# Prompt attention: value products of two steps taken in one visit of TensorE's 64-column arrangement

## The chip, the cores and the metric

The kernel runs on one core of a Trainium2 chip. A core has TensorE (PE in the profile; its weight loads are PEld), VectorE (DVE), ScalarE (ACT), GpSimd (POOL) and SyncE (SP), which issues most transfers. Each runs its own list of instructions in order and waits for the others through semaphores. The metric is the device time of one execution in microseconds; shorter is better.

## The reference

One inference step of a decoder layer for 1024 prompt tokens and 32 sample tokens. The part that matters here is the causal attention of the prompt: 8 heads, keys and queries of 96 numbers, values of 64, queries in blocks of 128.

```python
def masked_attend(q, k, v, q_pos, k_pos):
    s = jnp.einsum('...qhd,...khd->...hqk', q, k).astype(jnp.float32) * (QK_HEAD ** -0.5)
    s = jnp.where(k_pos[None, :] <= q_pos[:, None], s, NEG_INF)
    p = jax.nn.softmax(s, axis=-1).astype(v.dtype)
    return jnp.einsum('...hqk,...khd->...qhd', p, v)
```

Around it stand the projections, a gated mixer, attention of the sample tokens over a paged cache, cross-attention into 256 memory tokens, and a gated feed-forward part. All is float32; most matmuls are made of three products of a high and a low part.

## The kernel before

`phase2a` (L673) holds the prompt's attention. It is cut into 16 units (L721 and L722), numbered 0 to 15 here, each one head `h` and one half `G` of the tokens: four query blocks `e` of 128 tokens. With G = 0 a unit is short: its keys reach over 1 to 4 blocks, and it has three steps. With G = 1 it is long: 5 to 8 blocks, four steps (L997). In their order the units are (0,0), (1,0), (0,1), (1,1), (2,0), (2,1), (3,0), (3,1), (4,0), (4,1), (5,0), (6,0), (5,1), (7,0), (6,1), (7,1) as (h, G). So units 0, 1, 4, 6, 8, 10, 11 and 13 are short.

Of a unit, `scores` (L999) makes the scores of one query block on TensorE and VectorE takes them from PSUM with the mask and the maximum (L1015, L1019, L1021). `expo` (L1023) is ScalarE's exponential. `trans` (L1028) transposes the probabilities of one bank, four blocks of 128x128, on TensorE (L1032), and ScalarE copies them into a `pth` tile (L1034), of which there are six. `value` (L1036) multiplies a bank with the values (L1047): the stationary operand has 64 columns, the even query blocks' result goes to the first 64 partitions of the PSUM tile `o`, that of the odd ones to the other 64. A short unit has three banks, one in each step; a long one has seven, two in each of the first three steps and one in the last. `copy` (L1052) takes `o` to SBUF on VectorE, `out` (L1057) transposes it back, and VectorE scales it (L1064).

The order of TensorE, ScalarE, VectorE and GpSimd is written out by hand (L782 to L844). One step runs, in this order:

- in a unit's last step the exponentials that are pending
- `T`: the transposes of the step's banks (L811)
- the `out` that is due, then the other pending exponentials
- `jobs`: scores of the next unit's query blocks, or of the one after it (L818)
- `V`: the value products of the step before (L823 and L824), so a step's banks are transposed in one step and multiplied in the next
- `extra`: projections and head preparations (`proj_group`, `head_prep`, L985), weight sums on GpSimd, and steps that prepare the sample tokens

A *visit* here is a run of value products between other matmuls. The scores of a unit's last query block come one or two steps before the unit's own first step, since its first transposes need all four exponentials. Each bank's products accumulate into the unit's `o`, from its first bank to its last.

Of the kernel before, what the change touches and what calls it, by code (L numbers as in the profile page):

```python
# [154 lines left out]
class Net:  # L155
# [517 lines left out]
    def phase2a(self):  # L673
# [77 lines left out]
        for h in range(2, 8):  # L751
            b = 7 * (h - 1)
# [12 lines left out]
        def sample():  # L765
            self.close("lat")
            yield from self.sample_prep(pp)
            yield from self.pages_ahead()

        def mix():  # L770
            n = [self.t(p, [P, 4, 4, 96], F32, r, 2).rearrange("p m h d -> p (m h d)") for r in "kq"]
            hl = [x[:, 512:].rearrange("p (k n) -> p k n", k=4) for x in n]
            for k, _ in enumerate(self.mix_steps(
                pm, pp, 1, 0, 4, lambda i: b_all[:, i], lambda j: hl[j], lambda j: n[j // 2][:, :512], ("tp", 4)
            )):
                if k not in (1, 2, 8):
                    yield
                if k == 4:
                    yield

        E = mybir.EngineType
        with tc.manual_schedule(engines={E.PE, E.Activation, E.DVE, E.Pool}):  # L782
            for f in preps[0][0], preps[0][1], v1[0], norm[0], norm[1]:
                f()
            self.lows = []
            preps[1][0]()
            for e in range(4):
                units[0]["a"](e)
                if e == 1:
                    preps[1][1]()  # L790
                if e:
                    units[0]["e"](e - 1)
                    if e % 2:
                        v1[e // 2 + 1]()
            units[0]["e"](3)
            for f in norm[2:4]:
                f()
            self.flush()
            extra[0][:0] = norm[4:]
            extra[1][:0] = v1[3:]  # L800
            steps, outs, pend, V = [], {}, [], []
            self.sums = []
            t = 0
            for n, u in enumerate(units):
                for k, banks in enumerate(u["steps"]):
                    self.flush()
                    if k == len(u["steps"]) - 1:
                        for f in pend:
                            f()
                        pend = []  # L810
                    for b in banks:  # L811
                        u["T"](b)
                    for f in outs.pop(t, []):
                        f()
                    for f in pend:
                        f()
                    pend = []
                    for w, e in jobs[t]:  # L818
                        w["a"](e)
                        pend.append(lambda w=w, e=e: w["e"](e))  # L820
                    self.flush()
                    self.flush_sums()
                    for f in V:  # L823
                        f()  # L824
                    V = [lambda u=u, b=b: u["V"](b) for b in banks]
                    if k == len(u["steps"]) - 1:
                        outs.setdefault(t + 2, []).append(u["copy"])
                        outs.setdefault(t + 3, []).append(u["out"])
                        if order[n] == (7, 0):
                            outs[t + 3].append(lambda: steps.append(mix()))  # L830
                    for f in extra[t]:
                        f()
                    t += 1
                    if t == 32:
                        steps.append(sample())
                    steps = [x for x in steps if next(x, 0) is None]
            self.flush()
            self.flush_sums()
            self.lows = self.sums = None
            for fs in [V] + [outs[t] for t in sorted(outs)] + [[]] * 4:  # L840
                for f in fs:
                    f()
                steps = [x for x in steps if next(x, 0) is None]
            assert not steps  # L844
# [146 lines left out]
    def head_unit(self, p, pp, h, G, s, c):  # L991
# [75 lines left out]

        u.update({"a": scores, "e": expo, "T": trans, "V": value, "copy": copy, "out": out})
        return u
# [1443 lines left out]
```

## Time and profile before

| what | value |
|---|---|
| runs, median of 3 | 1827.49 us (1826.86 to 1828.1) |
| span of the profiled execution, first to last instruction | 1823.1 us |
| median of the runs less that span | 4.4 us |
| granted TensorE clock, mean | 0.998 |
| VectorE, ScalarE, GpSimd busy | 74%, 51%, 39% |
| value products L1047: records, first and last start | 352, 208.0 to 397.9 us |
| transposes L1032 and copies L1034 of them | 288 and 80 |

The profile gives the span of its execution; the times of the runs also hold what lies before the first instruction and after the last. Each value product shows as two records of TensorE. Rows of the timeline are: start in us from the span's start, length in us, engine, line, operation, out<-in, shapes, how many in a row, and in brackets the idle time before it and what ended it. Matmuls overlap and their lengths are modelled, so work on TensorE is best read from one start to the next. The table by stretches gives the stretch, its length, busy time and instructions of PE, PEld, DVE, ACT and POOL, then the granted TensorE clock, the DMA share and GB/s.

### The profile page before, as it was taken

To read this page: it belongs to the slowest core of one execution; us is meant where nothing else is said; L and a number is where in the kernel's file an instruction comes from. 1 tells how busy PE (TensorE), PEld (TensorE's weight loads), DVE (VectorE), ACT (ScalarE), POOL (GpSimd) and SP (SyncE) were. 2 spreads that over 40 slices of the span, in tenths; PEclk is the share of its full clock that TensorE was granted. 3 is DMA by queue.
4 is the path that set the end of the run, shared out by engine and by line. 5 is a ranking of instruction groups with operands and counts; after the bars stand their busy time and mean duration, and the time that the engine had idled before them with its cause. 6 is when DMAs were issued, how large, how long until landed. Compare 5 with 4: busy or idle time off the path is not lost.

```text
span 1823.1 us, 39307 instructions
## 1 busy us (share of the span) xinstructions
PE 1800.6 (99%) x14226; PEld 1700.3 (93%) x14226; DVE 1349.6 (74%) x2796; ACT 921.5 (51%) x1910; POOL 703.0 (39%) x861
## 2 busy tenths in 40 slices
PE   9999999999999999999999999999999999999999
PEld 8999777779999999998899979999999999999999
DVE  7864767657778776777645767998888888888664
ACT  7435676766655555556433556533333333344442
POOL 1021655534545444544023010377667776400000
PEclk9999999999999999999999999999999999999999
DMA  8102354558866766664645156222222222595242
GB/s 323 47 18 70 117 176 127 165 181 227 220 201 189 202 189 181 178 180 127 194 152 188 36 197 196 71 71 94 83 71 71 83 71 85 152 325 162 85 149 78
DMA packets 153187, 261.18 MB, mean 143 GB/s; under 512 B 20897, under 2 KB 97538, under 8 KB 152994
## 3 DMA queue, kind: packets, MB, share of 16 engines
q1 hardware_dynamic: 152130, 257.63, 45.4%
q8 instruction: 112, 1.84, 0.4%
q10 hardware_dynamic: 864, 1.05, 0.2%
q14 instruction: 81, 0.66, 0.1%
HBM read 212.79 MB, written 45.82 MB: 142 GB/s over the span
## 4 chain that ended last, share of the span: by engine, by line
PE 81%; DVE 3%; ACT 1%; issue 1%; SPq 1%; POOL 1%; DMA 0%; DVEq 0%; ACTq 0%; POOLq 0%
PE s L186 22%; PE d L186 12%; PE b L186 8%; PE F L186 7%; PE X L186 7%; PE E L186 7%; PE A L186 3%; PE y L186 3%; PE o L1047 2%; PE o L1537 2%; PE tp L1032 1%; PE tp L186 1%; PE s L1422 1%; PE tp L985 1%; PE t L186 1%
## 5 line engine op out<-in xcount | busy, mean ns | idle before, releaser
L186 PE MATMUL s<-w2h,ch 128*128 128x256 f32 x1018 | 301.9, 297 | 0.5 <-ACT S L1425 0.5
L186 PE MATMUL s<-w2h,cl 128*128 128x256 f32 x1018 | 293.2, 288 | 0.0
L186 PE MATMUL s<-w2l,ch 128*128 128x256 f32 x1018 | 292.9, 288 | 0.0
L186 PEld LDWEIGHTS s<-w2h,ch 128*128 128x128 f32 x1018 | 191.5, 188 | 8.9 <-issue 3.7
L186 PEld LDWEIGHTS s<-w2l,ch 128*128 128x128 f32 x1018 | 191.7, 188 | 0.0
L186 PEld LDWEIGHTS s<-w2h,cl 128*128 128x128 f32 x1018 | 191.3, 188 | 0.0
L1458 DVE TENSOR_REDUCE ss<-sq 128x16 f32<-128x1024 f32 x128 | 155.3, 1213 | 29.8 <-ACT sq L1455 29.4
L1407 POOL TENSOR_TENSOR cl<-cT,ch 128x512 fp32r<-128x512 f32 x64 | 83.5, 1304 | 185.6 <-ACT ch L1403 185.4
L1455 ACT ACTIVATE sq<-s 128x512 f32<-128x512 f32 x128 | 76.6, 598 | 82.7 <-PE s L186 82.7
L1452 ACT ACTIVATE sq<-s 128x512 f32<-128x512 f32 x128 | 76.9, 601 | 75.9 <-PE s L186 70.9
L201 ACT CAST a<-brb 128x528 fp32r<-128x528 f32 x77 | 48.8, 634 | 110.5 <-PE d L186 104.6
L186 PE MATMUL d<-a,w 128*128 128x264 f32 x768 | 95.2, 284 | 0.0
L202 DVE TENSOR_TENSOR a<-brb,a 128x528 fp32r<-128x528 f32 x77 | 54.1, 704 | 55.2 <-ACT a L201 55.1
L186 PEld LDWEIGHTS d<-a,w 128*128 128x128 f32 x768 | 94.3, 188 | 0.0
L2149 POOL TENSOR_TENSOR lo<-s,hi 128x1024 fp32r<-128x1024 f32 x20 | 64.0, 3200 | 45.7 <-ACT hi L2148 45.7
L186 PE MATMUL mm<-whi,xh 128*128 128x256 f32 (+3 forms) x272 | 77.1, 285 | 0.0
L2204 ACT COPY a<-A 128x264 f32<-128x264 f32 x43 | 16.1, 375 | 120.6 <-PE A L186 114.2
L186 PE MATMUL mm<-wlo,xh 128*128 128x256 f32 (+3 forms) x272 | 76.8, 285 | 0.1
L186 PE MATMUL mm<-whi,xl 128*128 128x256 f32 (+3 forms) x272 | 76.8, 286 | 0.0
L1403 ACT CAST ch<-cT 128x512 fp32r<-128x512 f32 x128 | 73.5, 629 | 0.0
L2270 POOL TENSOR_TENSOR cv<-cv,row 128x1056 f32<-128x1056 f32 x22 | 65.1, 2960 | 21.0 <-ACT cv L2269 21.0
L186 PE MATMUL d<-a,hi 128*128 128x264 f32 x552 | 72.0, 284 | 0.0
(755 smaller groups left out, 6348.1 us busy)
## 6 DMA issues: line engine op xcount, KB each, us to landing
cT<-cT SPq DMA_DIRECT2D x256, 160.0 KB, 2.8
ck<-ck SPq DMA_DIRECT2D x256, 144.0 KB, 3.4
raw<-w_up SPq DMA_DIRECT2D x44, 512.0 KB, 3.5
wsumd<-wsum SPq DMA_DIRECT2D x26, 512.0 KB, 3.9
actd<-cv SPq DMA_DIRECT2D x44, 264.0 KB, 2.4
brb<-actd SPq DMA_DIRECT2D x44, 264.0 KB, 5.7
wsum<-w_down SPq DMA_DIRECT2D x22, 512.0 KB, 3.8
raw<-wsumd SPq DMA_DIRECT2D x20, 512.0 KB, 3.7
```

The source lines that it names most:

```text
L186: x = self.nc.tensor.matmul(out, l, r, start=first and i == 0, stop=last and i == len(seq) - 1)
L201: first = {"act": nc.scalar.copy, "pool": nc.gpsimd.tensor_copy, "dve": nc.vector.tensor_copy}[eng](hi, src)
L202: low = lambda: nc.vector.tensor_tensor(lo, src, hi, ALU.subtract)
L1047: nc.tensor.matmul(u["o"][g : g + 64, o : o + m * P], s["v"][:, j, h % 4], th[:, z * P : (z + m) * P], start=j == 0, stop=b == len(banks) - 1,
L1403: nc.scalar.copy(d["h"][:, k], src[k])
L1407: (nc.vector if k else nc.gpsimd).tensor_tensor(d["l"][:, k], src[k], d["h"][:, k], ALU.subtract)
L1452: nc.scalar.activation(sq[:, 0], ps[:, :, n0 : n0 + 256], AF.Square)
L1455: nc.scalar.activation(sq[:, 1], pt.rearrange("p (e d) -> p e d", e=2), AF.Square)
L1458: yield lambda: nc.vector.tensor_reduce(s["ss"][:, g0 : g0 + 2].rearrange("p e (z h) -> p z e h", z=2), sq.rearrange("p z e (h d) -> p z e ...
L1537: nc.tensor.matmul(s["o"][j * 32 : j * 32 + 32], S[:, q * 4 + j], d["ck"][:, j, :257], start=q == 0 and j > 0, stop=q == 7)
L2149: eng.tensor_tensor(lo, src, hi, ALU.subtract)
L2270: nc.gpsimd.tensor_tensor(cv, cv, row, ALU.mult)
```

## The change

The list `V` of value products is no longer run in every step. It is run in the first step of a unit (k = 0), and in a long unit also in its third (k = 2); between those, the products of further steps are appended to it. A long unit's banks 0 to 3 are multiplied in its third step and its banks 4 to 6 in the first step of the next unit; a short unit's three banks all in the first step of the next unit, after that step's transposes and scores. What is left after the last unit is run at the end as before.

```diff
@@ -820,9 +820,11 @@
                         pend.append(lambda w=w, e=e: w["e"](e))
                     self.flush()
                     self.flush_sums()
-                    for f in V:
-                        f()
-                    V = [lambda u=u, b=b: u["V"](b) for b in banks]
+                    if k == 0 or k == 2 and len(u["steps"]) == 4:
+                        for f in V:
+                            f()
+                        V = []
+                    V += [lambda u=u, b=b: u["V"](b) for b in banks]
                     if k == len(u["steps"]) - 1:
                         outs.setdefault(t + 2, []).append(u["copy"])
                         outs.setdefault(t + 3, []).append(u["out"])
```

## The prediction

> **What bounds the kernel now.** I read the page's busy times first, then the groups of instructions by line for the stretch 205 to 400 us (the stage that the change touches), then who waited for whom there, then the timeline around single units.
>
> ```profile
> PE 1800.6 (99%) x14226; PEld 1700.3 (93%) x14226; DVE 1349.6 (74%) x2796; ACT 921.5 (51%) x1910; POOL 703.0 (39%) x861
> ...
> L1047 PE MATMUL o<-pth,v 128*64 128x256 f32 (+1 forms) x352 | 47.0, 358 | 0.6 <-ACT pth L1034 0.6
> L1032 PE MATMUL tp<-ident,pr 128*128 128x128 f32 x285 | 43.1, 280 | 3.9 <-ACT pr L1024 2.8 <-DVE qTl L208 1.0
> ...
> PE s L186 <- DVE pr L1019: 2.0, 6, 1.2
> ```
>
> TensorE is the bound of the whole kernel, so time won or lost on it in this stage reaches the end unless a wait takes it up. The value products (L1047) are 47.0 us of the 195. The next row is the one to watch: the transposes of the probabilities (L1032) already wait 3.9 us, 2.8 of them for the exponentials (L1024). TensorE has other work to do while ScalarE and VectorE finish a softmax, but at some units not enough. The value products are part of that other work.
>
> **What a visit costs.** Two visits of the 64-column arrangement with their neighbours:
>
> ```profile
> 251.01 0.39 PE L186 MATMUL s<-kTl,qTh 96*128 96x512 f32 x1
> 251.25 0.39 PE L186 MATMUL s<-kTh,qTl 96*128 96x512 f32 x1
> 251.56 1.08 PE L1047 MATMUL o<-pth,v 128*64 128x256 f32 x8
> 252.58 0.64 PE L985 MATMUL tp<-ident,k 128*96 128x128 f32 x4
> ...
> 267.06 0.65 PE L1047 MATMUL o<-pth,v 128*64 128x256 f32 x4
> 267.64 0.44 PE L186 MATMUL tp<-wqh,cqh 128*128 128x384 f32 x1
> 267.92 0.33 PE L186 MATMUL tp<-wql,cqh 128*128 128x384 f32 x1
> 268.09 0.34 PE L186 MATMUL tp<-wqh,cql 128*128 128x384 f32 x1
> ```
>
> Start to start, eight records take 1.02 us (251.56 to 252.58) and four take 0.58 (267.06 to 267.64): four more cost 0.44, so 0.14 of each visit is fixed. Entering costs 0.07 (0.31 from the score before it, where equal scores follow each other after 0.24). The first matmul after it is late by 0.11 where it is a projection (0.28 where its like take 0.17); of a transpose the merged row does not show it. A visit removed is worth 0.21 to 0.32 us; I take 0.3, as most of what follows a visit is seen to start late.
>
> **The change part by part.** No instruction is added or taken away; only the place of value products in TensorE's order changes. Sixteen units run, eight short (three steps, visits after steps 0, 1, 2 each one step later) and eight long (four steps). A short unit has three visits and keeps one, a long one has four and keeps two: 8 x 2 + 8 x 2 = 32, less one at the end, where the last unit's two visits stand side by side already. Gross, 31 x 0.3 = 9.3 us faster. No DMA and no instruction of another engine moves; the scores, transposes and exponentials keep their order. The probability tiles (`pth`, six of them) are held longer: six at once at step 2 of a long unit. The copy that wants the seventh stands behind the visit in TensorE's order anyway, so it adds no wait. VectorE's copy of the result (L1054) waits for the longer visit one step on, with the next unit's score reductions queued behind it; extras and transposes lie between in most units, so I cost it at nothing, and up to 0.3 us where there are none.
>
> What counts is the work that moves past a wait. Here is unit 8 (short) and the start of unit 9:
>
> ```profile
> 322.08 0.39 PE L186 MATMUL s<-kTh,qTl 96*128 96x512 f32 x1
> 322.40 0.65 PE L1047 MATMUL o<-pth,v 128*64 128x256 f32 x4
> 322.83 0.75 DVE L1015 CUSTOM_DVE_ANT_0 pr<-s,cmask,nm 128x512 f32<-128x512 f32 x1
> 322.98 0.44 PE L1032 MATMUL tp<-ident,pr 128*128 128x128 f32 x2
> ...
> 323.57 0.86 PE L1047 MATMUL o<-pth,v 128*64 128x128 f32 x6
> 323.62 0.21 DVE L1021 TENSOR_SCALAR nm<-nm,rq 128x1 f32<-128x1 f32 x1
> 323.87 1.24 ACT L1024 ACTIVATE pr<-pr,nm,rq 128x1024 f32<-128x1024 f32 x1 [0.99 <-DVE nm L1021]
> 324.36 0.55 PE L1032 MATMUL tp<-ident,pr 128*128 128x128 f32 x3
> 325.26 0.77 PE L1032 MATMUL tp<-ident,pr 128*128 128x128 f32 x5 [0.35 <-ACT pr L1024]
> 326.65 0.44 PE L1047 MATMUL o<-pth,v 128*64 128x128 f32 x4
> ```
>
> From unit 9's last score (322.08) a chain runs through VectorE (L1015, L1021) and ScalarE (the exponential, 323.87 to 325.11) to the fourth transpose of unit 9 (325.26). It takes 3.18 us and no link of it needs a value product. Under it TensorE does the visits at 322.40 and 323.57, 0.58 + 0.79 us, and waits 0.35 already. The change takes both away from here: TensorE stands idle for them, the transpose still starts at 325.26, and their work (0.44 for the four; 0.79 - 0.14 = 0.65 for the six) is done at 326.65. Nothing is won and **1.1 us is lost**. Units 6 and 13 are alike:
>
> ```profile
> 297.64 0.74 DVE L208 SCALAR_TENSOR_TENSOR qTl<-tp,ggq,qTh 96x512 fp32r<-96x512 f32 x1
> 298.44 1.09 PE L1032 MATMUL tp<-ident,pr 128*128 128x128 f32 x8 [1.04 <-DVE qTl L208]
> ...
> 375.70 1.24 ACT L1024 ACTIVATE pr<-pr,nm,rq 128x1024 f32<-128x1024 f32 x1 [1.37 <-DVE nm L1021]
> 377.09 0.76 PE L1032 MATMUL tp<-ident,pr 128*128 128x128 f32 x5 [1.10 <-ACT pr L1024]
> ```
>
> Unit 7's transposes wait 1.04 for VectorE, unit 14's 1.10 for an exponential: +1.1 and, since part of unit 13's chain follows projected work that comes earlier, +0.8. Unit 1 loses nothing, as the delay runs into a wait that is there anyway:
>
> ```profile
> 229.81 0.44 PE L1047 MATMUL o<-pth,v 128*64 128x128 f32 x4
> ...
> 233.53 0.47 PE L186 MATMUL s<-kTh,qTh 96*128 96x448 f32 x1 [1.20 <-DVE pr L1019]
> ```
>
> The other four (units 0, 4, 10, 11) lie between -0.6 (both visits' price won) and +1.1 (all their cover missed). I take +0.5 each, nearest the three that the rows show, as ScalarE or VectorE is close behind in all of them. Short units: 1.1 + 1.1 + 0.8 + 0 + 4 x 0.5 = **+5.0**.
>
> Long units, third visit (ten records, about 1.35 us with its ends) moved past the next unit's transposes. Entering a short unit there is room, entering a long one there is not:
>
> ```profile
> 312.38 0.82 ACT L1024 ACTIVATE pr<-pr,nm,rq 128x512 f32<-128x512 f32 x1
> 314.75 1.30 PE L1047 MATMUL o<-pth,v 128*64 128x256 f32 x10
> 317.19 0.60 PE L1032 MATMUL tp<-ident,pr 128*128 128x128 f32 x4
> ...
> 388.79 1.23 ACT L1024 ACTIVATE pr<-pr,nm,rq 128x1024 f32<-128x1024 f32 x1
> 390.16 0.77 PE L1032 MATMUL tp<-ident,pr 128*128 128x128 f32 x5 [0.48 <-ACT pr L1024]
> ```
>
> At unit 8 the exponential ends at 313.20 and its transposes start at 317.19, 4.0 us later: the 1.35 fits and 0.3 is won. Four of seven are such; one of these gains only what the full VectorE before 298.44 gives back, so 3 x -0.3 = -0.9. The others enter with little room (unit 15 above already waits 0.48). They lie between -0.3 and +1.1; I take +0.5 each, just above the middle because the one shown waits: +1.5. Sum **+0.6**. First visits of long units (eight records) move only past transposes and scores of their own unit: -0.3 each where buffers are free. In the tail (the last unit, below) and in two or three others the transposes of the result or of the queries wait for ScalarE, and the gain is lost there: 5 x -0.3 = -1.5, the rest +0.3: **-1.2**.
>
> ```profile
> 392.88 1.14 PE L1047 MATMUL o<-pth,v 128*64 128x256 f32 x8 [0.56 <-ACT pth L1034]
> 395.03 0.41 PE L1060 MATMUL tp<-ident,oc 128*128 128x128 f32 x2
> ...
> 398.20 1.53 PE L1701 MATMUL tp<-ident,b_all 128*128 128x128 f32 x12
> ```
>
> 5.0 + 0.6 - 1.2 = +4.4 us on the profiled span of 1823.1, so 1827.5. The median of the runs, 1827.49, lies 4.4 above that span, which I add: **1831.9**. By bounds, from the median: all gained, 1827.5 - 9.3 = 1818.2; every uncertain unit missed (four short and three long at +1.1, no first visit won), 1827.5 + 3.0 + 4.4 + 3.3 - 0.9, about 1837.3.
>
> **A rule that speaks against it.** More idle time can also close TensorE's clock:
>
> ```profile
> 202.00:205.40 3.40, 2.31 (x15) 1.71 (x14) 2.85 (x8) 3.08 (x10) 2.66 (x10) 1.00 0.01 2
> ...
> 212.20:215.60 3.40, 2.02 (x10) 1.36 (x9) 2.33 (x6) 1.44 (x3) 0.73 (x2) 1.00 0.43 136
> 215.60:219.00 3.40, 3.40 (x11) 2.60 (x9) 2.25 (x10) 0.00 (x0) 0.22 (x1) 0.53 0.65 197
> 219.00:222.40 3.40, 3.40 (x16) 2.69 (x16) 1.77 (x5) 1.21 (x3) 3.16 (x5) 0.50 0.45 151
> ```
>
> After a stretch with 2.02 us busy of 3.40 the granted clock was about half for 6.8 us; a stretch with 2.31 did not do it. Entering units 14 and 7 TensorE would idle some 2.4 us (1.10 or 1.04 plus the 1.4 of two visits), entering unit 9 1.7, so such a stretch may be made. One closing is worth up to 3.4 us (half of 6.8), less what other engines' waits hide. The Trainium skill, "TensorE: Matmul & The Clock Gate", section "Part 1: The HAM clock gate", says that the clock falls to half after one idle window of about 3.4 us; by that rule gaps of 2.4 us would not close it and this rival falls away. The row at 212.2 disagrees: that stretch was not wholly idle.
>
> **The rivals.** (1) *The visits were not needed as cover*: ScalarE and VectorE, given the same scores sooner, finish sooner. It decides from the point where, in the short units, the last exponential ends 1 us or more nearer to the last score than now; then 4 to 9 of the 9.3 us are won: 1818 to 1823.8, **0.15**. For it: at unit 8's start 4.0 us are free; against it: the waits at 298.44, 325.26, 377.09. (2) *Gain and loss cancel*: the four unread short units win and the long ones too, 1823.9 to 1831.1, middle 1828.5, **0.36**. (3) *The forecast*: short units lose their cover, 1831.2 to 1834.5, **0.33**. (4) *The clock closes once or twice more*, decided by whether a 3.4 us stretch falls to about 2 us of work: 1832 + 3 = 1835, to 1838, **0.16**. The change does do what it says: each kept visit is taken once, as the list is emptied only at those steps.
>
> **Numbers.** The forecast and rival 4 are one mechanism, lost cover, and are likelier together than any other; 1831.9 is its time without the clock. Range 1823.5 to 1837.5, which leaves out most of rival 1 and the end of rival 4. About 0.2% (3.7 us) is what a measurement of this kernel can tell from no change. Faster 0.15, same 0.36, slower 0.49.
>
> **What would show it.** Right: 25 or fewer visits of L1047 on the timeline; the idle time of L1032 before exponentials grown from 2.8 to some 10 us, most at units 7, 9 and 14; busy time of L1047 hardly changed; the stage's end near 402.6 instead of 398.2. Wrong: no growth of that wait (rival 1), or a granted clock below 1 in a stretch after 230 us (rival 4).

## The result and the profile after

The changed kernel takes **1836.27 us** (median of 5 runs, 1834.06 to 1840.49) against 1826.95 (5 runs, 1825.14 to 1828.1): 9.3 us more, ratio 1.0052, 95% interval 1.0041 to 1.0063. Lines from L825 on stand two higher than before: the transposes of the probabilities are L1034, their exponentials L1026, the value products L1049.

The page of the changed kernel (its share of busy time), then its groups of TensorE's instructions by line from 205 to 415 us, then who waited for whom there (us in all, times, longest):

```profile
span 1838.8 us, 39305 instructions
...
PE 1805.0 (98%) x14226; PEld 1712.5 (93%) x14226; DVE 1352.4 (74%) x2796; ACT 921.4 (50%) x1910; POOL 698.6 (38%) x861
...
L1034 PE MATMUL tp<-ident,pr 128*128 128x128 f32 x285 | 45.2, 289 | 10.9 <-ACT pr L1026 8.0 <-DVE qTl L208 2.8
L1049 PE MATMUL o<-pth,v 128*64 128x256 f32 (+1 forms) x352 | 44.1, 373 | 0.0
...
PE tp L1034 <- ACT pr L1026: 8.0, 7, 2.3
```

The profiled execution is the slowest of the five, so its 15.7 us over the span before are not all the change's. Still the place is plain: the idle time ahead of the transposes rose from 3.9 to 10.9 us, that for the exponentials from 2.8 to 8.0, in seven waits of up to 2.3. On the other side the busy time of the value products fell from 47.0 to 44.1.

Where the waits stand shows in the timeline of the changed kernel. The rows with L1034 at 303.24, 324.46, 333.45 and 387.90 are the transposes at the start of units 7, 8, 9 and 14; L1049 at 306.41 and 403.15 are two visits with what stands behind them; L1703 is the first work behind the stage:

```profile
303.24 1.97 PE L1034 MATMUL tp<-ident,pr 128*128 128x128 f32 x8 [2.11 <-DVE qTl L208]
...
306.41 2.83 PE L1049 MATMUL o<-pth,v 128*64 128x256 f32 x14
309.18 0.91 PE L987 MATMUL tp<-ident,k 128*96 128x128 f32 x4
...
324.46 0.60 PE L1034 MATMUL tp<-ident,pr 128*128 128x128 f32 x4
...
333.45 1.16 PE L1034 MATMUL tp<-ident,pr 128*128 128x128 f32 x5 [1.71 <-ACT pr L1026]
...
387.90 1.01 PE L1034 MATMUL tp<-ident,pr 128*128 128x128 f32 x5 [2.26 <-ACT pr L1026]
...
403.15 1.52 PE L1049 MATMUL o<-pth,v 128*64 128x256 f32 x14
404.60 1.96 PE L1034 MATMUL tp<-ident,pr 128*128 128x128 f32 x16
...
411.36 1.53 PE L1703 MATMUL tp<-ident,b_all 128*128 128x128 f32 x12
```

Entering units 7, 9 and 14 TensorE stands 2.11, 1.71 and 2.26 us, where it stood 1.04, 0.35 and 1.10 before. Unit 8's first transposes are 7.27 us later than before (317.19 to 324.46), unit 9's 8.19 (325.26 to 333.45): 0.92 lost in one unit. The end of the stage moved from 398.20 to 411.36, 13.2 us.

A second thing shows in two visits of 14 records. From start to start the one at 403.15 takes 1.45 us and the one at 306.41 takes 2.77. The second ran at half clock. The table by stretches of the changed kernel, cut at the clock's own steps of 3.41 us (columns as before: busy time and count of PE, PEld, DVE, ACT, POOL, granted clock, DMA share, GB/s):

```profile
210.82:214.23 3.41, 1.33 (x5) 0.64 (x5) 1.66 (x5) 3.17 (x8) 2.35 (x4) 1.00 0.45 154
214.23:217.65 3.42, 3.23 (x10) 2.79 (x11) 1.97 (x8) 0.00 (x0) 0.00 (x0) 0.50 0.89 273
217.65:221.06 3.41, 3.41 (x11) 2.27 (x12) 2.22 (x8) 0.00 (x0) 1.71 (x3) 0.50 0.57 168
221.06:224.47 3.41, 3.41 (x20) 2.64 (x17) 0.16 (x1) 0.42 (x1) 3.18 (x5) 0.50 0.41 141
...
227.89:231.30 3.41, 1.79 (x13) 1.10 (x12) 1.53 (x3) 3.41 (x9) 1.84 (x3) 1.00 0.64 221
231.30:234.71 3.41, 3.41 (x15) 2.77 (x16) 1.20 (x6) 1.21 (x3) 1.41 (x3) 0.50 0.81 258
...
299.57:302.98 3.41, 1.45 (x11) 1.01 (x9) 3.23 (x11) 1.67 (x4) 3.33 (x4) 1.00 0.00 0
302.98:306.39 3.41, 3.15 (x14) 2.96 (x14) 1.11 (x6) 1.85 (x6) 3.10 (x6) 0.50 0.21 73
306.39:309.80 3.41, 3.41 (x18) 2.27 (x18) 0.65 (x3) 0.00 (x0) 1.35 (x2) 0.50 0.45 131
309.80:313.22 3.42, 3.42 (x28) 3.00 (x27) 1.10 (x3) 2.30 (x6) 1.27 (x2) 1.00 0.77 257
...
330.29:333.70 3.41, 1.70 (x12) 1.17 (x11) 1.95 (x7) 2.54 (x5) 3.17 (x6) 1.00 0.39 147
333.70:337.11 3.41, 3.41 (x19) 2.81 (x19) 1.66 (x7) 1.17 (x2) 3.17 (x10) 0.50 0.48 159
...
384.90:388.31 3.41, 1.15 (x9) 0.73 (x9) 2.46 (x8) 1.88 (x6) 0.00 (x0) 1.00 0.79 231
388.31:391.73 3.42, 3.42 (x18) 2.71 (x18) 1.27 (x5) 1.13 (x2) 0.00 (x0) 0.51 0.66 194
```

A *closing* here is a time at half clock. Before each stands a stretch with 1.15 to 1.79 us of TensorE work. Four of the five closings stand behind short units (1, 6, 8, 13) and are new. The one at 214 was there before for 6.8 us and lasts 10.2 now. In all the stage holds 27.3 us at half clock where it held 6.8. So two losses lie over each other, idle time and a slower clock that the idle time brings. The experiments take them apart.

### The profile page after: what moved, and what is told of

The parts are those of the page before. It is cut to its first block, busy times and chain, and to the rows that moved or that the text cites. A ratio compares the mean times of both kernels' runs of the same rounds, so it can differ in the third digit from the quotient of the medians.

```text
span 1838.8 us, 39305 instructions
## 1 busy us (share of the span) xinstructions
PE 1805.0 (98%) x14226; PEld 1712.5 (93%) x14226; DVE 1352.4 (74%) x2796; ACT 921.4 (50%) x1910; POOL 698.6 (38%) x861
## 4 chain that ended last, share of the span: by engine, by line
PE 76%; DVE 4%; DMA 2%; ACT 2%; SPq 1%; issue 1%; POOL 1%; DVEq 0%; POOLq 0%; ACTq 0%
PE s L186 20%; PE d L186 12%; PE b L186 8%; PE F L186 7%; PE X L186 7%; PE E L186 7%; PE A L186 3%; PE y L186 3%; PE o L1539 2%; PE o L1049 1%; PE tp L1034 1%; PE tp L186 1%; PE s L1424 1%; SPq L1377 1%; PE t L186 1%
```

## The experiments

Theory 1: both losses come from the short units, whose value products were the cover of the next unit's softmax, the work that TensorE did while it was under way. Rivals: the long visits of the long units hold up what stands behind them (theory 2); the clock alone loses the time (theory 3); the change would win if only its shape were better. Line numbers of the kernels with filling transposes stand two or more higher still.

**Long units alone.** The short units' visits stay in every step.

```diff
-                    if k == 0 or k == 2 and len(u["steps"]) == 4:
+                    if len(u["steps"]) == 3 or k in (0, 2):
```

> Only the long units' visits are joined (4 to 2); short units multiply in every step as before. Lost cover in short units (theory 1): 15 visits fewer at 0.3 us, a part of it lost where a long unit follows a long one: 1825 to 1828, no more than 1.5 us from the kernel before, and one closing of the clock, as before. Long visits delay the scores and reductions behind them (theory 2): 3 us or more slower than before, 1830 up. The clock alone makes the loss (theory 3): 1823 to 1825, as no cover is charged.

Measured: 1824.07 us (11 runs) against 1826.99 (24 runs), ratio 0.9987 (0.9978 to 0.9996), 2.9 us faster. That is faster than theory 1 said and in the range of theory 3, so this run alone does not tell these two apart. Part of it may be the clock, whose mean was 0.9984 in these runs and 0.9976 in those before, at most 1.5 us. Joining visits is not a loss in itself. The timeline of this kernel shows the price of a visit:

```profile
251.43 1.95 PE L1049 MATMUL o<-pth,v 128*64 128x256 f32 x16
253.30 0.64 PE L987 MATMUL tp<-ident,k 128*96 128x128 f32 x4
```

Sixteen records in one visit take 1.87 us from start to start. Two visits of eight took 1.02 each, so 0.17 is saved inside; the entry and the late start behind the visit come on top. That long visits hold up the work behind them falls.

**Short units alone.** The long units' visits stay in every step.

```diff
-                    if k == 0 or k == 2 and len(u["steps"]) == 4:
+                    if len(u["steps"]) == 4 or k == 0:
```

> Only the short units' visits are joined (3 to 1). Theory 1: nearly the whole loss is here, 5 us of lost cover and 1 to 5 of half clock: 1833 to 1837, with the waits of the transposes for exponentials at 6 us or more and more than one stretch of half clock. Theory 2 (long visits): the visits of short units hold 14 records at most, so less than half of the loss: 1828 to 1831.

Measured: 1838.44 us (5 runs), ratio 1.006 (1.0046 to 1.0074), 11.4 us slower, above the 1833 to 1837 of theory 1. All of the loss, and more, is in the short units. The mean granted clock of these runs is 0.9934, that of the runs before 0.9976.

**First visits of the long units alone.** The third visits go back to their own step.

```diff
-                    if k == 0 or k == 2 and len(u["steps"]) == 4:
+                    if len(u["steps"]) == 3 or k != 1:
```

> Only the first visit of each long unit is joined to its second; the third stays where it was, and short units are untouched: 8 visits fewer. Theory 1: nothing moves past a wait for an exponential, 1.2 to 2.4 us faster than before: 1824.5 to 1826. Theory 2: slower than before by 1 us or more.

Measured: 1824.84 us (11 runs), ratio 0.9991 (0.9982 to 1.0), 2.15 us faster for eight visits, 0.27 each (by the interval, 0 to 0.4), at the same mean clock as before (0.9977 and 0.9976). The third visits add another 0.8 (1824.84 to 1824.07), within the scatter of the runs and within what their clocks differ by (0.9977 to 0.9984, at most 1.3 us).

**The gaps filled.** The whole change, but where a short unit's products were taken away, transposes of the identity that take about as long are put there:

```diff
+                    if k and len(u["steps"]) == 3:
+                        u["fill"]((5, 7)[k - 1])
                     V += [lambda u=u, b=b: u["V"](b) for b in banks]
...
+        def fill(m):
+            if "o" not in u:
+                u["o"] = self.t(pp, [P, 512], F32, "o", 2)[:, :256]
+            for _ in range(m):
+                nc.tensor.transpose(u["o"][:, :P], self.ident, self.ident)
```

> The changed kernel, and where the two visits of a short unit were taken away stand 5 and 7 transposes of the identity (about 0.55 and 0.76 us) that nobody reads; the value products stay joined. TensorE is kept at work while it would wait. Theory 1 with the clock as a second part: the lost cover stays, the added closings of the clock go: 1830 to 1833, 3 to 6 us faster than the changed kernel, one stretch of half clock. Theory 3 (the clock alone): back to 1827 or below. If the clock costs nothing: 1836 or slower, as work is added.

Measured: 1831.72 us (8 runs), ratio 1.0024 (1.0013 to 1.0034). TensorE does more, and the kernel is 4.6 us faster than the change without the filling (1836.27). The waits of this kernel, the stretches around units 7 and 14, and the end of the stage:

```profile
PE tp L1036 <- ACT pr L1028: 5.0, 6, 1.2
PE tp L1036 <- DVE qTl L208: 2.0, 3, 1.4
```

```profile
299.33:302.74 3.41, 2.43 (x24) 2.15 (x26) 2.26 (x10) 2.47 (x6) 3.17 (x5) 1.00 0.03 6
302.74:306.15 3.41, 3.41 (x30) 2.70 (x27) 1.23 (x4) 1.19 (x3) 2.02 (x3) 1.00 0.45 152
...
377.84:381.25 3.41, 2.25 (x20) 2.00 (x18) 2.88 (x10) 2.04 (x5) 0.00 (x0) 1.00 0.68 207
381.25:384.66 3.41, 3.40 (x28) 2.73 (x29) 1.52 (x6) 1.29 (x3) 0.00 (x0) 1.00 0.64 189
```

```profile
403.19 1.53 PE L1711 MATMUL tp<-ident,b_all 128*128 128x128 f32 x12
```

The longest wait is 1.4 instead of 2.3 us, the emptiest stretches there hold 2.43 and 2.25 us of work, and the clock stays at 1.00 behind them. Of the closings in the stage only the one at 214 is left, 6.8 us long, and the stage ends at 403.19 instead of 411.36. The mean granted clock of its runs is 0.9978 (the changed kernel's 0.9934, that of the kernel before, in the runs beside it, 0.9976).

How much of the 9.3 us is the clock's? Filling wins back 4.6. That is about the least, since the filling transposes are work of their own and cost time where there is no gap for them. The most can be estimated from the mean granted clock: 0.0042 less over 1836 us is 7.7 us, if all of it reaches the end. So the clock accounts for some 4.6 to 7.7 us, and the other 1.6 to 4.7 are lost cover, less what the joined visits win. That the clock alone loses the time falls: with the clock as before, the transposes still wait 7.0 us where they waited 3.9, and the short units alone lost 11.4 us at a clock that explains 7.7 at most.

**Short units alone, gaps filled.** The edits of the second and the fourth experiment together.

> Only the short units are joined, with the 5 and 7 transposes of the identity in place of their two visits; long units as before. The lost cover by itself, without clock and without the long units' gain. From the runs so far (fill 4.7 above before, long_only 2.9 below it) it should be 7.6 us slower than before: 1834.5, 1833 to 1836. If the long units' gain and the short units' loss did not add (the long ones then gave cover back): 1830 to 1832, the forecast's +5.

Measured: 1833.14 us (7 runs) against 1827.24 (29 runs), ratio 1.003 (1.0019 to 1.0042): 5.9 us at the clock of before, lost cover together with what the filling costs. From the other side, the 11.4 us of the short units alone less the 7.7 that the clock explains at most leave 3.7. So the short units' lost cover is 3.7 to 5.9 us, already less what their joined visits win. The filling is worth 5.5 here (11.4 less 5.9), about as much as in the whole change. 5.9 less the 2.9 that the long units win would be 3.0, where the fourth experiment found 4.7; the intervals, about 2 us to either side, don't tell these apart.

**Gaps filled by place.** First only behind the four units whose gaps closed the clock in the profile of the changed kernel, then only in the other four:

```diff
-                    if k and len(u["steps"]) == 3:
+                    if k and len(u["steps"]) == 3 and n in (1, 6, 8, 13):
```

> The changed kernel with the filling transposes (nobody reads their result) only in the short units 1, 6, 8 and 13, after which its profile shows a closing of TensorE's clock inside the stage. If a closing belongs to one gap, and comes where one stretch of 3.41 us (on a fixed grid within an execution) has less than about 1.9 us of TensorE work, these four fills remove the closings at 231, 303, 334 and 388, and the time is that of the kernel with all eight filled: 1830.5 to 1833.0, about 4.5 below the changed kernel. If the clock answers to the idle time of the whole stage, half of the fills gives about half of the gain: 1833.5 to 1835.

```diff
-                    if k and len(u["steps"]) == 3:
+                    if k and len(u["steps"]) == 3 and n in (0, 4, 10, 11):
```

> The changed kernel with the filling transposes only in the other short units 0, 4, 10 and 11. If a closing belongs to one gap, nothing is helped but perhaps the closing at 214, whose gap stands behind unit 0: 1835 to 1838, and a profile with the closings near 300, 331 and 386 still there. If the clock answers to the idle time of the whole stage, half of the gain: 1833.5 to 1835. If instead the filling transposes win time by something other than the clock, it is won here as well, about 2 us.

Measured, against 1826.41 us (14 runs): 1831.23 (8 runs), ratio 1.0026 (1.0016 to 1.0036), for the first; 1836.58 (6 runs), ratio 1.0056 (1.0043 to 1.0068), for the second. Four fills win as much as eight, and the other four alone win nothing. The clock of the first is below that of the kernel with eight fills (0.9964 against 0.9978, at most 2.6 us), so the other four fills seem to win some clock beside these and to cost about as much. It is single gaps that count, not the stage's idle time as a whole. The stretches of the first kernel, then of the second:

```profile
296.82:300.23 3.41, 2.05 (x18) 1.84 (x17) 3.23 (x11) 1.97 (x6) 3.25 (x5) 1.00 0.00 0
300.23:303.65 3.42, 3.42 (x32) 2.81 (x32) 1.26 (x8) 1.34 (x3) 3.19 (x5) 1.00 0.34 115
...
354.85:358.26 3.41, 2.26 (x24) 2.01 (x22) 3.04 (x10) 2.63 (x8) 2.72 (x4) 1.00 0.45 133
358.26:361.67 3.41, 3.41 (x18) 2.07 (x18) 1.51 (x8) 0.33 (x1) 1.83 (x3) 0.50 0.67 229
```

```profile
297.52:300.93 3.41, 1.60 (x14) 1.40 (x14) 2.79 (x8) 1.99 (x5) 3.17 (x5) 1.00 0.00 0
300.93:304.34 3.41, 3.41 (x32) 2.80 (x31) 1.07 (x6) 1.34 (x3) 3.17 (x5) 1.00 0.45 154
...
379.43:382.84 3.41, 1.14 (x9) 0.71 (x8) 2.67 (x9) 2.04 (x5) 0.00 (x0) 1.00 0.55 159
382.84:386.26 3.42, 3.42 (x15) 2.75 (x16) 1.23 (x5) 1.19 (x3) 0.00 (x0) 0.50 0.63 185
```

Two details were not as expected. The second kernel's profile has the closings near 331 and 386 (here 328.2 and 382.8) but none near 300, where a stretch with 1.60 us of work left the clock open. The first has a closing at 358.3 behind 2.26 us of work. The limit is not sharp.

**Other shapes.** Three attempts at more than the long units alone give. The first joins a short unit's first two visits in its own last step; the second also keeps a long unit's third visit in its place where a long unit follows. The third has the order of before, and nine filling transposes ahead of unit 1's first scores, to keep the clock open at 215:

```diff
-                    if k == 0 or k == 2 and len(u["steps"]) == 4:
+                    if k in (0, 2):
```

> The rule run at k = 0 and k = 2 for every unit: long units as in the change, short units multiply their first two steps at their last step, ahead of the next unit's transposes, and the third behind the unit. No cover of a short unit's wait goes but the price of one visit. Lost cover: the short units' loss is gone, 1821 to 1824, at or up to 3 us below the long units alone. If it is the joining as such that costs in short units, not the place past the wait: 1827 to 1831.

```diff
-                    if k == 0 or k == 2 and len(u["steps"]) == 4:
+                    if k in (0, 2) or (k == 3 and order[n + 1 if n < 15 else n][1]):
```

> As the rule k = 0 and k = 2 for every unit, but a long unit that is followed by a long one multiplies in its last step too, ahead of the transposes that wait there. Lost cover: 0 to 2 us faster than that rule, 1820 to 1823.5. If the third visits cost nothing there: the same as that rule or 0.9 us slower (three visits more).

```diff
+                    if n == 1 and k == 0:
+                        u["fill"](9)
                     for w, e in jobs[t]:
```

> The kernel before, with nine transposes of the identity, 1 us, in the idle ahead of unit 2's first scores (212.2 to 213.2), and no other edit. If idle time in a stretch of 3.4 us closes the clock, the closing of 6.8 us at 215.8 is gone and the kernel is 1 to 3.4 us faster: 1823.5 to 1826. If the clock falls for another reason: half clock of 6.8 us there as before, and 1827 to 1828.

Measured, against 1827.24: 1825.8 us, ratio 0.9996 (0.9987 to 1.0005); 1824.99, ratio 0.9989 (0.998 to 0.9998); 1826.24, ratio 0.9994 (0.9985 to 1.0003), 11 runs each. All three miss what was expected: the first lies between its two ranges, the second 1.5 us above its range, the third just above its own. None beats the long units alone in the median, though the second's runs had the lower clock (mean 0.9973 against 0.9984), so which of these two orders is better isn't settled. In the profile of the third the closing at 215 is gone, but one of 3.4 us stands at 232.4 instead, so it says little of what the first is worth. **The fastest median is that of the long units alone**, 1824.07 us, below both kernels of the comparison, by 0.04 to 0.22% of the one before.

## Why the prediction was right, and where it was off

The forecast was 1831.9 us, the range 1823.5 to 1837.5; 1836.27 is slower, as forecast, and lies in the range, but it is the time that the text gave its fourth rival (1835 to 1838, a chance of 0.16). The direction and the lost cover came as argued. That the time lies inside the range is in part luck: its upper end was made of units that lose all their cover at full clock, and the kernel came near it by closings of the clock.

- **Price of a visit**, 0.3 us out of 0.21 to 0.32: eight visits won 2.15 us, 0.27 each. It holds, within a wide interval.
- **Short units lose their cover**, +5.0: 3.7 to 5.9 measured without the clock. The single gaps were right too. The text gave some 2.4 us entering units 14 and 7 and 1.7 entering unit 9; the trace has 2.26, 2.11 and 1.71. Unit 8 was to lose 1.1 and lost 0.92. Unit 1, costed at nothing because its delay runs into a wait that is there, was wrong in another way: the stretch behind it fell to 1.79 us of work and the clock closed at 231.3.
- **Long units**, +0.6 for the third visits and -1.2 for the first: -0.8 and -2.15 measured, together -2.9 (ratio 0.9978 to 0.9996, up to 1.5 us of it perhaps the clock) instead of -0.6. The sign of the first visits was right; the third visits were sized by the one start of a unit that was seen to wait, and that loss was given to two more, which the runs don't bear out. The text also miscounts: by the order of the units five of the seven long units lead into a short one, not four, so its own prices give about -0.2 for the third visits (-1.2 and 2 x +0.5).
- **The sum without the clock** was 1831.9, and with the gaps filled the chip gave 1831.72. Against the median of its own before, the filled kernel is 4.7 us slower, where the text had 4.4. Much of this closeness is luck: 4.7 holds what the filling costs, the change without the clock lies anywhere from 1.6 to 4.7, and the parts measured one at a time add up to 3.0 (5.9 less 2.9).
- **The clock** is the step that failed. The text saw the limit (2.02 us of 3.40 closed it, 2.31 did not) and the gaps, with their lengths, but asked whether one or two more closings would come and gave that 0.16. Cut at the clock's own steps, the stretch that closed it (212.39 to 215.80) holds 2.19. The sum of the text's own numbers said more than it made of them: 3.4 less a gap of 2.4 leaves 1.0 us of work, well below the limit, wherever such a gap falls into one stretch. Three of its gaps were 1.7 us or longer, and all three closed the clock, unit 1's as a fourth. Rival 4 should have been the forecast. What one closing costs was about right: a closing of 6.8 us was priced at up to 3.4. In the two profiles, filling takes 20.5 us of half clock and 8.2 us of time out of the stage (411.36 to 403.19), so 6.8 us cost at least about 2.7. The number of closings was not.
- **The rule of the Trainium skill**, "TensorE: Matmul & The Clock Gate", section "Part 1: The HAM clock gate", by which the clock falls after an idle window of about 3.4 us, would have kept the clock open here, if idle means no work. The runs decide against that reading: stretches with 1.14 to 1.82 us of work closed it. The same section calls the window free-running, 3413 ns long; with that the rows agree, as closings within one execution stand whole multiples of 3.41 us apart (from 302.98 to 388.31: 85.33, 25 of them).
- **What would show it**: the timeline has 24 rows of L1049 where before has 55 of L1047, one for each visit. The wait for exponentials grew to 8.0 of the 10 named, most at units 7, 9 and 14 when the one for VectorE is added. L1049's busy time fell by 2.9 where "hardly changed" was said. The stage's end is 411.36 where 402.6 was said, and a clock below 1 after 230 us was the mark named for rival 4.

What stays open: of the 15.7 us between the two profiled spans 2.5 come after the stage. A closing of 3.4 us at 886.6, which the profile of before lacks, can explain 1.7 of them; the kernel with the first visits alone, faster than before, has one at 872.4, so such a closing needs no lost cover. What the closing at 215, which both kernels have, costs was not settled, nor where between 4.6 and 7.7 us the clock's share lies.

## What to carry to other kernels

Before small pieces of work are joined to save their fixed price, ask what each piece covers: here 0.27 us a visit was won where other work stood in the gap, and 3.7 to 5.9 us over eight units, some 0.5 to 0.7 a unit, were lost where the pieces were the gap's only filling. Then hold each gap that results against the clock's stretch: 3.41 us less the gap is the work left in it, and below about 1.9 us a closing has to be put into the forecast itself, not beside it. Where a gap can't be avoided, cheap work in it that nobody reads can pay (4.6 us here), though the kernel with the gaps filled was still 4.7 us slower than before the change.

## What the runs showed of the hardware

The prediction had two rows for the limit of the clock; the runs give many. Cut at the steps of 3.41 us on which its closings lie, the stretches at full clock from about 205 to 410 us in the profiles of the changed kernel, the one before and the ten experiments are 678. Of the 18 with less than 1.9 us of TensorE work, 16 were followed by half clock; of the 23 from 1.9 to 2.4 us, four, three of these at about 212 us; of the 637 with more, none. A closing lasts one to three such stretches. Where the steps fall differs between executions, so whether a gap of 1.6 to 2.3 us lies within one stretch is a matter of its place. That may be why the five runs of the changed kernel spread over 6.4 us with granted clocks of 0.992 to 0.995, the slowest run at the lowest; no trace here shows it, as only one of the five has one. Place does not explain all: the wait of 1.81 us that ended at 300.11 in the kernel with the other four units filled lies wholly inside the stretch 297.52 to 300.93 above, and the clock stayed open. Outside this stage the limit does not hold: before the closing at 886.6 stand stretches with 3.15 and 3.42 us of TensorE work.
